# Two layers of a hybrid decoder trunk: the large SBUF tiles begin on a multiple of 2 KB

## Chip, cores and metric

The kernel runs on one NeuronCore of a Trainium2 chip. The metric is device time in microseconds of one execution: 2147.09 us before the change, the median of three runs.

## What is computed

512 tokens of width 1024 pass through two layers, all in float32. Each layer adds half a SwiGLU to x, then a mixer of three groups of heads whose inputs come from one common projection, then half of another SwiGLU. A last RMSNorm closes the trunk.

```python
for l in range(DEPTH):                                   # DEPTH = 2, D_MODEL = 1024, D_FF = 2816
    x = x + 0.5 * swiglu(rmsnorm(x, ffn1_norm[l]), ffn1_w_gate[l], ffn1_w_up[l], ffn1_w_down[l])
    z = rmsnorm(x, mix_norm[l]) @ w_in[l]
    ...
    y = jnp.concatenate([y_s5, y_hg, y_nsa], axis=-1).astype(x.dtype)
    x = x + y @ w_out[l]
    x = x + 0.5 * swiglu(rmsnorm(x, ffn2_norm[l]), ffn2_w_gate[l], ffn2_w_up[l], ffn2_w_down[l])
return rmsnorm(x, final_norm)
```

Here `swiglu(h, wg, wu, wd)` is `(silu(h @ wg) * (h @ wu)) @ wd`. The mixer's groups are a diagonal state-space model (S5), a gated linear recurrence (HGRN2) and sparse attention (NSA).

## The kernel before

Features lie on the 128 partitions and tokens along the free axis, so x is the tile `x` of 8 x 512 numbers on each partition (`consts`, L117). Products are taken to nearly the full precision of float32 by splitting both sides: a value is the sum of a part `hi` that the type float32r holds and the rest `lo`, and a product is three matmuls, hi x hi, hi x lo and lo x hi (`mm3`, lines 219 to 221). `norm_split` (L158 and L159) writes the split of x times the norm's gain into `xs`, of 2 x 8 x 512 numbers: first the eight `hi` tiles, then the eight `lo` tiles.

A weight tile comes from DRAM into one of four buffers `wraw` (L204, issued by SyncE), 4 KB on each partition; ScalarE casts it to `whi` (L213) and VectorE takes the difference to `wlo` (L214), three buffers each. Then `dense_x` runs over the eight k-tiles of 128 features: 24 matmuls of 128 rows by 512 columns with `whi` or `wlo` as the stationary operand and `xs` as the operand that streams past it, into one PSUM tile `pd`. The same three lines serve the second half of a SwiGLU, where the hidden layer `hb` (2 x 11 x 512 numbers) streams, and the mixer's output projection (`wout`), where its split results `y` stream. The last rows of the last SwiGLU (`finish`) stream 256 columns of `hb` at a time, with weights in tiles `fw` of their own.

The program goes through SwiGLU, mixer, SwiGLU for each of the two layers. A SwiGLU is done in two halves of 11 hidden tiles; each has 22 runs of `dense_x` and 8 rows of output. Beside the first SwiGLU of layer 0 and the second one VectorE computes the S5 tables of a layer from parameters; those have few matmuls, among them groups of four, L698 and L699, that stream `Rs` (256 columns) past weights `shm`. In the mixer several streams are emitted side by side, the projections (16 runs of `dense_x`), the three groups and the output projection.

SBUF addresses are given out by tile pools, one behind the other in the order in which the pools are opened, each pool as large as its buffers: first 16 KB and 128 bytes of each partition that the system and four constants take, then `res` (everything that lives through the program: gains, `x`, `xs`, the identity `idn`, small tables), `wp` (weights and norm statistics), `sm` (small columns), and behind them the pool of the stage that runs, a SwiGLU's (`r05`, `hb`, `ft`, `fw`) or the mixer's (46 buffers of 2 KB, `y` among them). `x` stands behind the gains, at 16384 + 128 + 224 = 16736, which is 8 x 2048 + 352, and `xs` 16 KB behind it.

Of the kernel before, what the change touches and what calls it, by code (L numbers as in the profile page):

```python
# [28 lines left out]
def drain(gen):  # L29
    """run a stream of steps to its end"""  # L30
    while True:
        try:
            next(gen)
        except StopIteration as e:
            return e.value


class Weave:
    """emits several streams side by side; each step tells its tensor-engine cost in us, weights share it out"""
# [7 lines left out]
    def run(self, until=None):  # L47
        """steps until stream `until` (or all) has ended"""
        while self.live:
            e = min(self.live, key=lambda t: (t[0], t[1]))  # L50
            self.now = e[0]
            try:
                e[0] += (next(e[3]) or 0.1) / e[2]
            except StopIteration:
                self.live.remove(e)
                if e[3] is until:
                    return
# [5 lines left out]
class Trunk:  # L63
    def __init__(self, ctx, tc, A):
        self.ctx, self.tc, self.nc, self.A = ctx, tc, tc.nc, A
        E = ctx.enter_context
        self.res = E(tc.tile_pool(name="res", bufs=1))
        self.wp = E(tc.tile_pool(name="wp", bufs=3))
        self.sm = E(tc.tile_pool(name="sm", bufs=8))
        self.pp = E(tc.tile_pool(name="pp", bufs=1, space=PSUM))  # L70
        self.dr = E(tc.tile_pool(name="dr", bufs=1, space=DRAM))
# [15 lines left out]
    NB = 46  # L87
    HT = ('pS', 'pv')

# [10 lines left out]
    def rsqrt(self, v, n):  # L100
        """v: AP [128, n] -> tile [128, n] holding v ** -0.5"""
        nc = self.nc
        i = self.s([128, n], "rsi", I32)
        nc.vector.tensor_scalar(i[:], v.bitcast(I32), 1, None, op0=OP.logical_shift_right)
        nc.vector.tensor_scalar(i[:], i[:], -1.0, float(0x5f3759df), op0=OP.mult, op1=OP.add)
        y = i[:].bitcast(F32)
        for _ in range(3):
            t = self.s([128, n], "rst")
            nc.vector.tensor_tensor(t[:], y, y, op=OP.mult)
            nc.vector.scalar_tensor_tensor(t[:], t[:], -0.5, v, op0=OP.mult, op1=OP.mult)  # L110
            y2 = self.s([128, n], "rsy")
            nc.vector.scalar_tensor_tensor(y2[:], t[:], 1.5, y, op0=OP.add, op1=OP.mult)
            y = y2[:]
        return y2

# [1 line left out]
    def consts(self):  # L117
# [3 lines left out]
        self.x = res.tile([128, KT, L], F32, name="x")  # L121
        self.xs = res.tile([128, 2, KT, L], F32R, name="xs")
# [26 lines left out]
    def norm_x(self, k, gi):  # L149
        """statistics of x tile k, and its split x*gain for the next products"""  # L150
        self.norm_sq(k)
        if gi is not None:
            self.norm_split(k, gi)
# [26 lines left out]
    def norm_rows(self):  # L180
        """rstd along the columns, the same on every partition"""
        nc = self.nc
        pb = self.rows(4)
        self.rbc = self.wp.tile([128, L], F32, tag="rbc", name="rbc", bufs=2)
        nc.scalar.copy(self.rbc[:], pb[:])
# [10 lines left out]
    def wload(self, src, n):  # L196
        """src: DRAM AP [128, n] -> (hi, lo) float32r tiles that add up to it exactly"""
        return self.wsplit(self.wraw(src, n), n)
# [24 lines left out]
    def dense_x(self, src, m=128, tag="pd"):  # L223
        """one tile of m output rows: sum over the 1024 features of w * (x * gain)"""
        h, lo = self.wload(src, KT * m)
        ps = self.pmt(name="pd", tag=tag)
        for k in range(KT):
            sl = slice(k * m, (k + 1) * m)
            self.mm3(ps[:m], h[:, sl], lo[:, sl], self.xs[:, 0, k], self.xs[:, 1, k], k == 0, k == KT - 1)
            if k % 2:  # L230
                yield 1.3
        return ps

# [1 line left out]
    def begin(self, fi, gi):  # L235
        """loads x and starts the first products of a SwiGLU on its tiles as they come"""
# [82 lines left out]
    def finish(self, fi, hb, r05, fp, out):  # L319
        """the last rows of the last SwiGLU and the final norm, 256 tokens after the other"""  # L320
# [41 lines left out]
    def advance(self, side, budget):  # L362
        """emits about `budget` us of a stream of vector work"""
# [39 lines left out]
    def exp_small(self, pool, x, n, name):  # L403
        """exp of [128, n] to float32's accuracy"""
# [21 lines left out]
    def params_small(self, pool):  # L426
        """S5: step sizes, exp(lambda dt) and the input gains; HGRN2: lower bounds (both layers)"""
# [19 lines left out]
        # lower bounds: cumsum(softmax) - softmax[0]  # L447
# [14 lines left out]
        # E = expm1(lr dt)  # L462
# [10 lines left out]
        # half angle w = (li dt mod 2 pi) / 2  # L473
# [26 lines left out]
        # a = mag (cos, sin); nr = Re(a) - 1  # L500
# [22 lines left out]
        def cmul(o, a, b):  # L523
            """complex product of (re, im) pairs"""
# [13 lines left out]
        # powers a^0 .. a^8, [128, n, 9]  # L538
# [10 lines left out]
        # unit phase of a^8, decay of a^8  # L549
# [18 lines left out]
    def params_layer(self, l, pool):  # L568
        """S5 matrices of a layer, to DRAM: V, Toeplitz, readout, phases"""
# [8 lines left out]
        # phases E^c, c = 0..63, of the chunk's 8 steps, layout [g, c]  # L578
        for hf in range(2):
# [9 lines left out]
            while w < 32:  # L589
                # E^(2w) = (E^w)^2, then columns 2w .. 4w-1 from 0 .. 2w-1  # L590
# [16 lines left out]
            # modulated values take [re; im] * C + [im; re] * (S, -S)  # L607
# [4 lines left out]
        # input matrices: BB = [re; im], BX = [-im; re] of g * b  # L612
# [18 lines left out]
        # readout matrices from c: D1 = [re; -im], C2 = [im; re]  # L631
# [3 lines left out]
        D1 = c1  # L635
# [3 lines left out]
        # powers in falling order, a^7 .. a^0  # L639
# [13 lines left out]
        def expand(out, X, Y, W, gsl, op):  # L653
            """out[., g, h, s] = X[., g, h] W0[., g, s] (op) Y[., g, h] W1[., g, s]"""
# [27 lines left out]
        # Toeplitz matrices of the 8 steps, from rows of the readout moved by 0 / 1 matrices  # L682
# [20 lines left out]
    def cmp_bias(self, l, pool):  # L703
        """contribution of the position vectors to the hidden layer of the block compression"""
# [38 lines left out]
    def s5_half(self, l, hf, u, U, W):  # L743
        """yields y = gelu(ssm + d u) * 2 for 8 groups, [channel, (s c)]"""
# [45 lines left out]
    def gelu2(self, y, p, n):  # L790
        """2 * gelu(y) of an SBUF AP [p, n]"""
# [12 lines left out]
    def s5_glu(self, l, y2):  # L804
# [4 lines left out]
        for m in range(2):  # L809
# [7 lines left out]
            # natural order of time, split  # L817
# [7 lines left out]
    def silu_ps(self, ps, name):  # L825
        """silu(ps * rstd)"""
# [25 lines left out]
    def hg_pair(self, l, pr, q, f, k, g, V, tag="pv"):  # L852
        """two heads; q, f, k, g: [2 x 64, t]"""
        nc = self.nc
        v = nc.vector
        # what the products of keys and queries keep: within 64 tokens, and blocks of 64, 128 and 256 to the next one
# [6 lines left out]
        def prod(K, Q, e):  # L863
            """keys against queries within each 64 tokens: [2 x 64 keys, 4, 64 queries]"""
# [15 lines left out]
        for lev in range(9):  # L880
# [16 lines left out]
            if lev < 8:  # L897
# [4 lines left out]
                # the last level reads the second half of Q and the first half of K alone  # L902
# [39 lines left out]
        # rms norm over the head's 64 values  # L942
# [29 lines left out]
    def cmp_in(self, ps):  # L972
        """[2 groups x 64, t] -> [64 | 64 shifted by one token, group, t]"""
# [14 lines left out]
    def cmp_hidden(self, l, kv, kk, w1):  # L988
        """both halves of a block in one product over its 16 tokens: rows (half, hidden), columns (group, chunk)"""
# [13 lines left out]
    def cmp_k(self, l, h2):  # L1003
        """compressed keys, stacked twice: [128, 64] with columns (group, block)"""
# [8 lines left out]
    def cmp_v(self, l, h2):  # L1013
        """compressed values, block diagonal by head pair: [4 x 32 blocks, pair, 2 x 64]"""
# [15 lines left out]
    def nsa_k(self, ps):  # L1030
        """[k_sl | k_wn] of a group -> for each: hi twice, lo twice on the partitions"""
# [15 lines left out]
    def nsa_q(self, ps):  # L1047
        """two heads -> [hi | lo] on the partitions for each, scaled, with the sign of a distance to the maximum"""
# [13 lines left out]
    def nsa_gates(self, g):  # L1062
        """sigmoid of the gates' logits, in place"""
# [5 lines left out]
    def bias_tile(self, h):  # L1069
        """row p, column c: minus the bias of distance p + 384 - c, read off along a skew of the lines of 640"""  # L1070
# [5 lines left out]
    def nsa_cmp(self, g, T, Q, kc, gates):  # L1076
        """gated and normalised weights of the compressed blocks, transposed: [4 x 32, t]"""
# [42 lines left out]
    def nsa(self, st):  # L1120
        """attention of all heads, one pipeline over (group, head pair, head, 128 queries)"""
# [16 lines left out]
        def scores(g, hp, i):  # L1138
            """weights of two heads and 128 queries, [head][selected, window]"""
# [86 lines left out]
    def dense_tok(self, W, n, name, gates=None):  # L1226
        """n columns of w_in (256, and 24 more for the gates) as [token, 4, 256]"""
# [28 lines left out]
    def row_halves(self, V):  # L1256
        """copies of V that keep tokens 0-63 / 64-127 of each 128 and hold zeros for the others"""
# [131 lines left out]
def _layout(inp):  # L1389
# [4 lines left out]
    def tiles(w, m):  # L1394
        """[K, M] -> [M / m, 128, K / 128, m]"""
        K, M = w.shape
        return w.reshape(K // 128, 128, M // m, m).transpose(2, 1, 0, 3)
# [34 lines left out]
    # S5: [2 (re / im) x 64 states, group]  # L1432
# [19 lines left out]
    # constants of the shapes  # L1452
# [40 lines left out]
```

## Time and profile before

| | |
|---|---|
| median of 3 runs | 2147.09 us |
| lowest run | 2145.63 us |
| span of the profiled execution, first to last instruction | 2143.8 us |
| TensorE busy | 2121.0 us, 99% |
| VectorE busy | 1188.3 us, 55% |
| ScalarE busy | 785.9 us, 37% |
| GpSimd busy | 82.9 us, 4% |
| DMA | 209.11 MB, mean 98 GB/s |

PE stands for TensorE's matmuls and PEld for its weight loads, DVE for VectorE, ACT for ScalarE, POOL for GpSimd and SP for SyncE. Busy time is the union of an engine's instructions. Matmuls are pipelined, so that each one's duration overlaps the next one's start: how fast they follow each other is read from their starts. In a row, `pd<-xs,whi` says that a matmul writes `pd` and streams `xs` past the weights `whi`. One run of the three took 2792.54 us; the median isn't moved by it.

### The profile page before, as it was taken

Reading aid. Unit: us, or ns where it says so; the run is one execution under the profiler, and the core shown is the slowest. Engines: PE = TensorE matmul, PEld = TensorE weight load, DVE = VectorE, ACT = ScalarE, POOL = GpSimd, SP = SyncE. Lnnn points to the kernel's source line nnn. Section 1 sums busy time; section 2 is a strip of 40 time slices with the busy share of each in tenths; the row PEclk is TensorE's granted clock in tenths of the full one; section 3 lists DMA queues with packets and bytes.
Section 4 is the critical chain, followed back from the end, with each engine's and each line's share of the span. In section 5 each row is a group of like instructions: output and inputs, shape, how many; then the busy total and the mean of one; then the engine's idle time right before and its main releaser. Section 6 shows DMA issues by size and latency. Waiting matters only on the chain.

```text
span 2143.8 us, 28943 instructions
## 1 busy us (share of the span) xinstructions
PE 2121.0 (99%) x11192; PEld 1693.9 (79%) x11192; DVE 1188.3 (55%) x2653; ACT 785.9 (37%) x1455; POOL 82.9 (4%) x153
## 2 busy tenths in 40 slices
PE   8999999999999999999999999999999999999997
PEld 6888788877767888888888888888777678888886
DVE  7864535676765864543543343366866663334335
ACT  5222223445566422222332222233455653222221
POOL 1000000111000000000000000001100000000000
PEclk9999999999999999999999999999999999999999
DMA  5334433433101432422333233234321023233322
GB/s 191 114 95 129 129 132 95 142 115 100 50 16 50 143 111 94 154 89 80 107 98 91 81 114 94 77 112 139 105 78 50 26 79 93 82 93 112 94 77 71
DMA packets 69753, 209.11 MB, mean 98 GB/s; under 512 B 9272, under 2 KB 11912, under 8 KB 69616
## 3 DMA queue, kind: packets, MB, share of 16 engines
q1 hardware_dynamic: 58192, 172.19, 26.1%
q0 software_dynamic: 11280, 35.05, 4.8%
q8 instruction: 88, 1.44, 0.3%
q14 instruction: 49, 0.40, 0.1%
q10 hardware_dynamic: 144, 0.03, 0.0%
HBM read 194.63 MB, written 15.22 MB: 98 GB/s over the span
## 4 chain that ended last, share of the span: by engine, by line
PE 96%; issue 2%; DVE 1%; DMA 0%; POOL 0%; ACT 0%; SPq 0%; DVEq 0%; POOLq 0%
PE pd L219 27%; PE pd L221 27%; PE pd L220 27%; PE pno L1193 2%; PE ppt L1177 2%; PE psS L1154 2%; PE psS L1151 1%; PE plv L870 1%; PE psc L1090 1%; PE pd L1245 1%; PE pd L1246 1%; PE pho L940 1%; PE pd L1247 1%; PE pno L1196 0%; PE pY L779 0%
## 5 line engine op out<-in xcount | busy, mean ns | idle before, releaser
L213 ACT CAST whi<-wraw 128x1024 fp32r<-128x1024 f32 (+5 forms) x377 | 344.6, 915 | 1061.0 <-PE pd L220 743.6
L219 PE MATMUL pd<-xs,whi 128*128 128x512 f32 x1664 | 666.5, 401 | 6.4 <-ACT whi L213 6.3
L221 PE MATMUL pd<-xs,wlo 128*128 128x512 f32 x1664 | 660.9, 397 | 0.0
L220 PE MATMUL pd<-xs,whi 128*128 128x512 f32 x1664 | 660.1, 397 | 0.0
L214 DVE TENSOR_TENSOR wlo<-wraw,whi 128x1024 fp32r<-128x1024 f32 (+5 forms) x377 | 396.9, 1054 | 145.2 <-ACT whi L213 137.1
L219 PEld LDWEIGHTS pd<-xs,whi 128*128 128x128 f32 x1664 | 313.4, 188 | 86.4 <-ACT whi L213 6.3
L221 PEld LDWEIGHTS pd<-xs,wlo 128*128 128x128 f32 x1664 | 312.8, 188 | 76.1 <-issue 0.4
L220 PEld LDWEIGHTS pd<-xs,whi 128*128 128x128 f32 x1664 | 313.2, 188 | 74.6 <-DVE xs L159 1.2
L219 PE MATMUL pd<-hb,whi 128*128 128x512 f32 x682 | 266.0, 390 | 0.0
L221 PE MATMUL pd<-hb,wlo 128*128 128x512 f32 x682 | 265.5, 389 | 0.0
L220 PE MATMUL pd<-hb,whi 128*128 128x512 f32 x682 | 265.4, 389 | 0.0
L288 DVE TENSOR_TENSOR ft<-ft,pd 128x512 f32<-128x512 f32 x88 | 60.4, 686 | 263.6 <-PE pd L221 263.3
L282 DVE TENSOR_TENSOR ft<-pd,rbc 128x512 f32<-128x512 f32 x88 | 60.6, 690 | 201.8 <-PE pd L221 201.8
L221 PEld LDWEIGHTS pd<-hb,wlo 128*128 128x128 f32 x682 | 128.0, 188 | 26.9
L219 PEld LDWEIGHTS pd<-hb,whi 128*128 128x128 f32 x682 | 128.1, 188 | 26.4
L220 PEld LDWEIGHTS pd<-hb,whi 128*128 128x128 f32 x682 | 128.1, 188 | 26.3
L307 DVE TENSOR_TENSOR ft<-pd,r 128x512 f32<-128x512 f32 x62 | 42.8, 691 | 109.5 <-PE pd L221 109.2
L1161 ACT ACTIVATE P<-P,mx 128x128 f32<-128x128 f32 (+3 forms) x128 | 71.7, 561 | 51.9 <-DVE mx L1157 50.2
L1157 DVE CUSTOM_DVE_ANT_0 P<-Tb,psS 128x128 f32<-128x128 f32 (+3 forms) x128 | 60.7, 484 | 49.5 <-PE psS L1154 48.8
L290 DVE TENSOR_TENSOR hb<-ft,hb 128x512 fp32r<-128x512 f32 x88 | 60.1, 683 | 0.0
L283 ACT ACTIVATE ft<-ft 128x512 f32<-128x512 f32 x88 | 55.2, 628 | 5.6 <-DVE ft L282 5.3
L289 ACT CAST hb<-ft 128x512 fp32r<-128x512 f32 x88 | 54.7, 621 | 6.5 <-DVE ft L288 4.5
(388 smaller groups left out, 2156.8 us busy)
## 6 DMA issues: line engine op xcount, KB each, us to landing
wraw<-in_gu SPq DMA_DIRECT2D x175, 512.0 KB, 3.5
wraw<-in_dn SPq DMA_DIRECT2D x64, 384.0 KB, 3.0
wraw<-in_dn SPq DMA_DIRECT2D x64, 320.0 KB, 2.8
wraw<-in_win SPq DMA_DIRECT2D x32, 512.0 KB, 3.6
w<-sp POOLq DMA_DIRECT2D x32, 256.0 KB, 6.4
wraw<-in_wo SPq DMA_DIRECT2D x32, 256.0 KB, 2.6
Tb<-tbl POOLq DMA_DIRECT2D x16, 256.0 KB, 3.5
tbl<-ext POOLq DMA_DIRECT2D x1, 2560.0 KB, 19.4
```

The source lines that it names most:

```text
L213: nc.scalar.copy(h[:, sl], w[:, sl])
L214: self.mark = nc.vector.tensor_tensor(lo[:, sl], w[:, sl], h[:, sl].bitcast(F32), op=OP.subtract)
L219: nc.tensor.matmul(ps, wh, xh, start=first, stop=False)
L220: nc.tensor.matmul(ps, wh, xl, start=False, stop=False)
L221: nc.tensor.matmul(ps, wl, xh, start=False, stop=last)
L282: nc.vector.tensor_tensor(t[:], pg[:], rbc[:], op=OP.mult)
L283: nc.scalar.activation(t[:], t[:], AF.Silu)
L288: nc.vector.tensor_tensor(t2[:], t[:], pu[:], op=OP.mult)
L289: nc.scalar.copy(hb[:, 0, f], t2[:])
L290: nc.vector.tensor_tensor(hb[:, 1, f], t2[:], hb[:, 0, f].bitcast(F32), op=OP.subtract)
L1157: v.tensor_tensor_reduce(p[:, :n], T[g][2 * hp + e][:, L - n:], ps[e][:, :n], 1.0, 1e29, OP.add, OP.min, mx[:, 2 * e + b:2 * e + b + 1])
L1161: nc.scalar.activation(P[j][:, :n], P[j][:, :n], AF.Exp, bias=mx[:, j:j + 1], scale=-1.0, accum_out=sm_[:, j:j + 1])
```

## The change

The small pool `sm` is opened right behind `res`; `x` and `xs` leave `res` for a pool of their own, `big`, behind a tile of 192 bytes that nothing reads; `wp` follows. The sizes are such that `big` then begins at 24576, a multiple of 2 KB, and as the tiles behind it are multiples of 2 KB themselves, so do all that follow.

```diff
         self.res = E(tc.tile_pool(name="res", bufs=1))
+        self.sm = E(tc.tile_pool(name="sm", bufs=8))
+        self.al = E(tc.tile_pool(name="al", bufs=1))
+        self.big = E(tc.tile_pool(name="big", bufs=1))
         self.wp = E(tc.tile_pool(name="wp", bufs=3))
-        self.sm = E(tc.tile_pool(name="sm", bufs=8))
...
     NB = 46
+    ALIGN = 192
...
-        self.x = res.tile([128, KT, L], F32, name="x")
-        self.xs = res.tile([128, 2, KT, L], F32R, name="xs")
+
+        self.al.tile([128, self.ALIGN // 4], F32, name="al")
+        self.x = self.big.tile([128, KT, L], F32, name="x")
+        self.xs = self.big.tile([128, 2, KT, L], F32R, name="xs")
```

The rest of the diff takes comments out. Instructions, their order on each engine and what each waits for are the same before and after. The start addresses in a partition, as the program gives them out, with their remainders:

| tile | before | mod 64 | mod 2048 | after | mod 64 | mod 2048 |
|---|---|---|---|---|---|---|
| `x` | 16736 | 32 | 352 | 24576 | 0 | 0 |
| `xs` | 33120 | 32 | 352 | 40960 | 0 | 0 |
| `idn` | 65888 | 32 | 352 | 16736 | 32 | 352 |
| `wraw` (first of 4) | 71232 | 0 | 1600 | 73728 | 0 | 0 |
| `whi` (first of 3) | 91712 | 0 | 1600 | 94208 | 0 | 0 |
| `wlo` (first of 3) | 104000 | 0 | 1600 | 106496 | 0 | 0 |
| `hb` | 128832 | 0 | 1856 | 129024 | 0 | 0 |
| `ft` (first of 3) | 173888 | 0 | 1856 | 174080 | 0 | 0 |
| mixer tiles, `y` among them | 126784 + 2048 n | 0 | 1856 | 126976 + 2048 n | 0 | 0 |
| `fw` (first of 4) | 184128 | 0 | 1856 | 184320 | 0 | 0 |
| `Rs`, `shm` in layer 0 | 223008, 204576 | 32 | 1824 | 223200, 204768 | 32 | 2016 |
| `Rs`, `shm` in layer 1 | 218112, 199680 | 0 | 1024 | 218304, 199872 | 0 | 1216 |

Within a tile, a slice of 512 columns begins a multiple of 2 KB behind the tile's start, and a weight slice of 128 columns a multiple of 512 bytes. The four `fw` tiles lie 5632 = 11 x 512 bytes apart.

## Rows read from the trace of the kernel before

**Rows 1.** The page's part 1 and, of its part 2, TensorE's granted clock.
```profile
PE 2121.0 (99%) x11192; PEld 1693.9 (79%) x11192; DVE 1188.3 (55%) x2653; ACT 785.9 (37%) x1455; POOL 82.9 (4%) x153
...
PEclk9999999999999999999999999999999999999999
```
**Rows 2.** The page's part 4: the chain that ended last, by engine.
```profile
PE 96%; issue 2%; DVE 1%; DMA 0%; POOL 0%; ACT 0%; SPq 0%; DVEq 0%; POOLq 0%
```
**Rows 3.** Waits: who waited for whom, us in total, times, longest.
```profile
ACT whi L213 <- PE pd L220: 743.6, 232, 5.4
...
PE pd L219 <- ACT whi L213: 6.3, 1, 6.3
```
**Rows 4.** Groups by line: xcount, busy us, mean ns of one, idle before.
```profile
L219 PE MATMUL pd<-xs,whi 128*128 128x512 f32 x1664 | 666.5, 401 | 6.4 <-ACT whi L213 6.3
L221 PE MATMUL pd<-xs,wlo 128*128 128x512 f32 x1664 | 660.9, 397 | 0.0
L220 PE MATMUL pd<-xs,whi 128*128 128x512 f32 x1664 | 660.1, 397 | 0.0
...
L219 PE MATMUL pd<-hb,whi 128*128 128x512 f32 x682 | 266.0, 390 | 0.0
L221 PE MATMUL pd<-hb,wlo 128*128 128x512 f32 x682 | 265.5, 389 | 0.0
L220 PE MATMUL pd<-hb,whi 128*128 128x512 f32 x682 | 265.4, 389 | 0.0
```
**Rows 5.** Timeline, PE: start us, us, instruction; `xs` streams.
```profile
1850.05 0.39 PE L219 MATMUL pd<-xs,whi 128*128 128x512 f32 x1
...
1852.85 0.39 PE L219 MATMUL pd<-xs,whi 128*128 128x512 f32 x1
```
**Rows 6.** The same timeline where `hb` streams.
```profile
1240.09 0.39 PE L219 MATMUL pd<-hb,whi 128*128 128x512 f32 x1
...
1242.81 0.39 PE L219 MATMUL pd<-hb,whi 128*128 128x512 f32 x1
```
**Rows 7.** The same timeline where `y` streams.
```profile
693.93 0.39 PE L219 MATMUL pd<-y,whi 128*128 128x512 f32 x1
...
696.65 0.39 PE L219 MATMUL pd<-y,whi 128*128 128x512 f32 x1
```
**Rows 8.** Windows, PE on `xs`, then on `hb`: us, busy (xcount), clock, DMA share, GB/s.
```profile
1820.00:1880.00 60.00, 60.00 (x259) 1.00 0.27 84
...
1020.00:1070.00 50.00, 50.00 (x223) 1.00 0.35 107
```
**Rows 9.** Windows, `xs`, `hb`, `y`: us, PE, PEld, DVE, ACT, POOL busy, clock, DMA.
```profile
1850.00:1853.00 3.00, 3.00 (x14) 2.40 (x14) 1.15 (x2) 1.54 (x2) 0.00 (x0) 1.00 0.28 112
1240.00:1243.00 3.00, 3.00 (x15) 2.49 (x14) 2.21 (x3) 0.84 (x1) 0.00 (x0) 1.00 0.23 77
694.00:697.00 3.00, 3.00 (x15) 2.49 (x14) 2.84 (x5) 2.15 (x4) 0.00 (x0) 1.00 0.72 186
```
**Rows 10.** Timeline, PE, layer 1: four products on `Rs`, then `hb` again.
```profile
855.80 0.28 PE L698 MATMUL ptt<-Rs,shm 128*128 128x256 f32 x1
...
856.15 0.28 PE L699 MATMUL ptt<-Rs,shm 128*128 128x256 f32 x1
856.27 0.39 PE L219 MATMUL pd<-hb,whi 128*128 128x512 f32 x1
...
857.43 0.40 PE L221 MATMUL pd<-hb,wlo 128*128 128x512 f32 x1
```
**Rows 11.** Timeline, PE, the last stage: `hb` with weights `fw`, 256 columns.
```profile
2114.10 0.28 PE L219 MATMUL pd<-hb,fw 128*128 128x256 f32 x1
...
2115.18 0.28 PE L219 MATMUL pd<-hb,fw 128*128 128x256 f32 x1
```
**Rows 12.** Timeline, PE, layer 0: four products on `Rs`.
```profile
200.18 0.28 PE L698 MATMUL ptt<-Rs,shm 128*128 128x256 f32 x1
...
200.53 0.28 PE L699 MATMUL ptt<-Rs,shm 128*128 128x256 f32 x1
```

## The prediction

> **What bounds the kernel now.** I read the page's busy shares first, then the chain that ended last, then the costliest groups, and last single stretches of the timeline and of the windows. The busy shares put TensorE at 99% of the span, at a granted clock of nine tenths or more in all 40 slices [rows 1]. The chain that ended last is 96% TensorE [rows 2]. The waits between engines say the same: ScalarE's cast of the weights waits 743.6 us in total for TensorE to give a weight buffer back, while TensorE waits for that cast once, 6.3 us, at the start [rows 3]. So DMA, ScalarE and VectorE run ahead, and what they would gain or lose by a change of a few per cent is covered. What counts is the time from one matmul's start to the next one's; I call it the pitch. The busy time of a matmul (390 to 401 ns) is no use for that, since matmuls overlap.
>
> The groups name three lines, 219 to 221, the three products of each split weight with a split operand [rows 4]. All are 128 rows by 512 columns, on the same weight tiles (`whi`, `wlo`) and the same PSUM tile (`pd`), and differ in what streams past the weights. With `xs` they take 397 to 401 ns on the average, with `hb` 389 to 390. There are 3 x 1664 = 4992 of the first and 3 x 682 = 2046 of the second; by the code another 384 (8 rows of output x 8 tiles x 3 products x 2 layers) stream `y`.
>
> The pitch shows the difference plainly. With `xs`, from the product of line 219 that starts at 1850.05 to the one at 1852.85 there are 12 steps: 2.80 us / 12 = 233.3 ns [rows 5]. With `hb`, from 1240.09 to 1242.81, also 12 steps: 2.72 / 12 = 226.7 ns [rows 6]. With `y`, from 693.93 to 696.65: again 226.7 ns [rows 7]. Over longer stretches it stays: 259 matmuls touch a window of 60 us on `xs` and 223 one of 50 us on `hb` [rows 8]; a matmul of 390 ns that overlaps an edge is counted too, so about 1.7 are to be taken off, which leaves 60 / 257.3 = 233 and 50 / 221.3 = 226 ns. Other engines don't explain it: the stretch on `xs` has the least VectorE work of the three (1.15 us in 3, against 2.21 and 2.84) and less ScalarE and DMA work than that on `y`, and it is the slow one [rows 9].
>
> What sets `xs` apart is its address. `hb` and `y` start 1,856 bytes past a multiple of 2 KB, which is a multiple of 64. `xs` starts 352 bytes past one, which is 32 past a multiple of 64, and of the operands that stream 512 columns in the dense products it alone does. The size of the difference fits: 233.3 - 226.7 = 6.6 ns, and 16 columns of 4 bytes, that is 64 bytes, at 2.4 columns per ns are 6.7 ns. My reading is that each matmul on `xs` pays for one 64-byte piece more at its ends, 33 instead of 32. No row shows the piece itself.
>
> **The change part by part.** No instruction is added, removed or moved, and no wait changes; only start addresses do. `x` and `xs` go from 32 past a multiple of 64 to a multiple of 2 KB. Weight tiles go from 64 past a multiple of 512 to a multiple of 2 KB, `hb`, `y` and the other mixer tiles from 1,856 past one to one; these were on multiples of 64 before. The small tiles and the identity keep their place within 2 KB.
>
> *`xs` as the streaming operand.* I take the row of `hb` as its price after the change. 768 of the 4992 (16 tiles x 24 products x 2 layers) stand in the mixers, the other 4224 in the SwiGLU stages, where they follow each other for long stretches: 4224 x 6.6 ns = 27.9 us. In the mixers they alternate with small products of the other streams, and there even an aligned operand doesn't always reach 226.7: behind four products of another shape `hb` takes (857.43 - 856.27) / 5 = 232 ns a step [rows 10]. So the pitch has to settle after each interruption. For the mixers the gain lies between 0 and 768 x 6.6 = 5.1 us; between ends this close I take the middle, 2.5. The sum is 30.4 us.
>
> *`hb`, `y` and the weights, from one multiple of 64 to another.* I take nothing. What bounds it: from below, nothing suggests a price yet (see the third rival); from above, the products on `Rs` and its weights, which start on multiples of 512 in layer 1, run at (856.15 - 855.80) / 3 = 117 ns for 256 columns [rows 10], those on `hb` with `fw`, 320 past a multiple of 512, at (2115.18 - 2114.10) / 9 = 120 ns [rows 11]. So 3 ns a matmul might be gained. But they come in runs of four, which may not have settled, and in layer 0, where both start 32 past a multiple of 64, four of them take the same 117 (200.18 to 200.53, 3 steps in 0.35) [rows 12]. I stay with the long row.
>
> *`x` for VectorE and ScalarE, the DMAs' targets, `ft`, `rbc`.* Nothing: a cast that waits 743.6 us for TensorE [rows 3] hides whatever these gain or lose. With that cover gone a matmul would wait for its weights, as it does now only in the first 6.3 us.
>
> When the matmuls quicken, the weights have to come quicker: a tile of 24 products is used up in 24 x 226.7 = 5.4 us, not 5.6, which against waits of this size is little. So the span goes from 2143.8 to 2113.4 us. The median of the three runs, 2147.1, is 3.3 above the span; with the same 3.3 I forecast 2116.7, rounded to **2116.5 us, 1.4% less**. Within this case, from no gain in the mixers and 10% less elsewhere to full gain and 1 ns more per matmul, it could be 2108 to 2124.
>
> The Trainium skill has a rule that speaks against this. On the page "SBUF — State Buffer", section "Specifications (TRN2)", the memory's lines are 16 bytes. By that rule an offset of 32 is no worse than one of 0, the sum would be zero and the time 2147. The rows of `xs` against `hb` and `y` disagree with it, as long as address is what parts them.
>
> **The rivals.**
>
> *No change: `xs` is slow for another reason.* The matmuls settle into one of two rhythms, and `xs` falls into the slower by something that stays, such as its place in the lower half of the partition, or the 16 KB between its two halves. (The page's rule of 16-byte lines comes out here.) For it: an aligned `hb` can also run at 232 ns for a while [rows 10], so a slow rhythm needs no misalignment; and the four products on `Rs` in layer 0, 32 off, run at 117 ns as those of layer 1 do, which aren't [rows 10, 12]. Against it: `xs` never settles over stretches of 60 us, `hb` does within some ten steps, `y`, scattered over many buffers, settles too. Time: 2147.
>
> *Faster still.* Weights and operands that all start on 2 KB let every matmul settle lower. The nearest row for how far is 117 against 120 ns [rows 10, 11], 3 ns on each of 4992 + 2046 + 384 = 7422: 22 us more, 2094. Against it: `Rs` has 117 without such a start too [rows 12]. On the page "TensorE: Matmul & The Clock Gate" of the Trainium skill, section "Back-to-back issue gap", the gap is N/2.4 + 2.5 ns, 216 for 512 columns; no row here shows it, the best being 226.7. By that rule, as an estimate, the xs products would save 17 ns and the others 11, some 114 us, and the time would be about 2033.
>
> *Slower: the two streams collide.* TensorE reads the operand and the next weights at the same time. Their starts are 288 bytes apart modulo 512 with `xs` now, 256 with `hb` and `y`; after the change all are 0 apart, since weight slices are 512 bytes. If starts at the same place get in each other's way, no stream settles. The price is read from `hb` unsettled, 232 against 226.7 ns: 2430 x 5.3 = 13 us on `hb` and `y`, and nothing gained on `xs`: 2160; with 5.3 on `xs` too, 2186. It decides from 30.4 us / 7422 = 4.1 ns per matmul on. Against it: `hb` and `fw` are 0 apart modulo 512 already, and run at 120 ns, 13.3 above 256 / 2.4 = 106.7, just as the settled 226.7 is 13.3 above 512 / 2.4 [rows 11].
>
> **How the numbers follow.** The forecast gets 0.80: three operands, two of them aligned, one difference, and its size. No change gets 0.09, faster still 0.07, collision 0.04. The forecast's own spread, 2108 to 2124, holds most of its 0.80; to reach 8 in 10 I widen it towards the neighbours, mostly down, where a small gain of the aligned streams would add to the forecast: 2098 to 2128. A measurement of this kernel tells about 2% from no change, here 43 us, 2104. Faster by over that: the second rival, 0.07, and 0.02 of the forecast's lower edge. Slower by over 2%: 0.02, the costlier half of the collision. The rest, 0.89, is within.
>
> **What would show it.** In the profile after, steps on `xs` of 226.7 ns and a mean of 389 to 390 ns for lines 219 to 221 (their numbers move by a few) would show the main step right; 233.3 would show it wrong, and with it the whole sum. `hb` and `y` should keep 226.7: less would be the second rival, 230 or more the third. TensorE should stay at 99%, and the wait of the cast for TensorE should stay in the hundreds. If `xs` reaches 226.7 and the span falls by much less than 30 us, the mixers or the supply of weights have taken it back, and TensorE's waits for `whi` would have grown.

## The result, and the profile after

The changed kernel takes 2116.97 us in the median of four runs (2116.30 to 2117.48), against 2146.49 for the kernel before in four runs (one of 2792.54, the others 2145.63 to 2147.09); the ratio is 0.9862, with an interval of 0.9848 to 0.9877. That is 1.4% less: under the 2% from which a run is called faster here, but clear of noise, as the interval lies below 1. The forecast was 2116.5. The span of the profiled execution went from 2143.8 to 2114.5 us.

The profile's page of the kernel after, parts 1 and 2 (compare [rows 1]):

```profile
span 2114.5 us, 28943 instructions
...
PE 2091.4 (99%) x11192; PEld 1695.1 (80%) x11192; DVE 1188.1 (56%) x2653; ACT 786.7 (37%) x1455; POOL 82.8 (4%) x153
```

TensorE has lost 29.6 us of busy time with the same 11192 matmuls and is still at 99%. The other engines' totals stand within 1 us. So the time came out of matmuls. Which ones, the costliest groups tell (part 5 of the same page; the changed file has five lines more ahead of the products, so lines 224 to 226 are lines 219 to 221 of before, [rows 4]):

```profile
L224 PE MATMUL pd<-xs,whi 128*128 128x512 f32 x1664 | 657.8, 395 | 6.7 <-ACT whi L218 6.1
L226 PE MATMUL pd<-xs,wlo 128*128 128x512 f32 x1664 | 652.2, 392 | 0.0
L225 PE MATMUL pd<-xs,whi 128*128 128x512 f32 x1664 | 650.8, 391 | 0.0
...
L224 PE MATMUL pd<-hb,whi 128*128 128x512 f32 x682 | 265.8, 390 | 0.0
L226 PE MATMUL pd<-hb,wlo 128*128 128x512 f32 x682 | 265.4, 389 | 0.0
L225 PE MATMUL pd<-hb,whi 128*128 128x512 f32 x682 | 265.4, 389 | 0.0
```

The three groups on `xs` have come down from 397 to 401 ns to 391 to 395; those on `hb` have not moved. What counts is the step from start to start. The timeline of TensorE in the kernel after, at three stretches (`y`, `hb`, `xs`; compare [rows 5 to 7]; start us, us, instruction):

```profile
690.14 0.39 PE L224 MATMUL pd<-y,whi 128*128 128x512 f32 x1
...
692.86 0.39 PE L224 MATMUL pd<-y,whi 128*128 128x512 f32 x1
...
1240.04 0.39 PE L224 MATMUL pd<-hb,whi 128*128 128x512 f32 x1
...
1242.76 0.39 PE L224 MATMUL pd<-hb,whi 128*128 128x512 f32 x1
...
1819.89 0.39 PE L224 MATMUL pd<-xs,whi 128*128 128x512 f32 x1
...
1822.62 0.39 PE L224 MATMUL pd<-xs,whi 128*128 128x512 f32 x1
```

Each pair is 12 steps apart. `y` and `hb` keep 2.72 / 12 = 226.7 ns. `xs` takes 2.73 / 12 = 227.5 here, where the starts are rounded to 10 ns, instead of 233.3; over its long stretches the mean step is 226.7. Summed over all starts of the trace, the steps that begin on a product with `xs` come to 1155.7 us after and 1184.6 before: 28.9 of the span's 29.3 us. All the other matmuls together differ by less than 0.3 us.

The supply keeps up. From the waits of the kernel after (who waited for whom, us in total, times, longest; compare [rows 3]):

```profile
ACT whi L218 <- PE pd L225: 703.6, 230, 5.3
...
PE pd L224 <- ACT whi L218: 6.1, 1, 6.1
```

The cast of the weights has 40 us less to wait for TensorE, and TensorE still waits for it once, at the start.

### The profile page after: what moved, and what is told of

The parts are those of the page before. It is cut to its first block, busy times and chain, and to the rows that moved or that the text cites. A ratio compares the mean times of both kernels' runs of the same rounds, so it can differ in the third digit from the quotient of the medians.

```text
span 2114.5 us, 28943 instructions
## 1 busy us (share of the span) xinstructions
PE 2091.4 (99%) x11192; PEld 1695.1 (80%) x11192; DVE 1188.1 (56%) x2653; ACT 786.7 (37%) x1455; POOL 82.8 (4%) x153
## 3 DMA queue, kind: packets, MB, share of 16 engines
q1 hardware_dynamic: 58192, 172.19, 27.1%
## 4 chain that ended last, share of the span: by engine, by line
PE 98%; DVE 1%; issue 0%; DMA 0%; ACT 0%; SPq 0%; POOL 0%; DVEq 0%; POOLq 0%
PE pd L224 28%; PE pd L226 27%; PE pd L225 27%; PE pno L1198 2%; PE ppt L1182 2%; PE psS L1159 2%; PE psS L1156 1%; PE plv L875 1%; PE pd L1250 1%; PE pd L1251 1%; PE pd L1252 1%; PE psc L1095 1%; PE pho L945 0%; PE pno L1201 0%; PE pY L784 0%
## 5 line engine op out<-in xcount | busy, mean ns | idle before, releaser
L224 PE MATMUL pd<-xs,whi 128*128 128x512 f32 x1664 | 657.8, 395 | 6.7 <-ACT whi L218 6.1
L226 PE MATMUL pd<-xs,wlo 128*128 128x512 f32 x1664 | 652.2, 392 | 0.0
L225 PE MATMUL pd<-xs,whi 128*128 128x512 f32 x1664 | 650.8, 391 | 0.0
```

Source lines behind the costliest of these rows:

```text
L224: nc.tensor.matmul(ps, wh, xh, start=first, stop=False)
L225: nc.tensor.matmul(ps, wh, xl, start=False, stop=False)
L226: nc.tensor.matmul(ps, wl, xh, start=False, stop=last)
```

## Experiments

The prediction had a mechanism (what counts is where the operand begins, modulo 64) with the right size and no row that showed it. The change moves all large tiles at once, so its success tells little about which of them mattered. In what follows a tile's start is its remainder as the table of the change gives it, and the *distance* is the start of the streaming operand minus the start of the weights it streams past. The edits that move tiles add unused tiles of 32 to 192 bytes, or resize one, and add no instruction. The kernel before is the reference in every ratio.

**Is 2 KB needed, or a multiple of 64?** In the kernel before, 32 unused bytes ahead of `x` and 32 behind `xs`. `x` and `xs` then start 384 past a multiple of 2 KB, weights 1664, `hb` and `y` 1920: all multiples of 64.

```diff
+        res.tile([128, 8], F32, name="pa")
         self.x = res.tile([128, KT, L], F32, name="x")
         self.xs = res.tile([128, 2, KT, L], F32R, name="xs")
+        res.tile([128, 8], F32, name="pb")
```

> The kernel before, with 32 unused bytes ahead of x and 32 behind xs: x and xs start on a multiple of 64 (384 past a multiple of 2 KB), all behind them moves by 64 bytes and stays off 2 KB (weights 1664 past one, hb and y 1920 past one). Theory (what counts is that the streaming operand starts on a multiple of 64): xs steps at 226.7 ns as after the change, time 2117 us, give or take 2. Rival 1 (it takes the 2 KB, for xs or for the weights beside it): xs stays at 233.3 ns, 2147 us. A value between, 2125 to 2140, would say that both count.

Measured: 2116.83 us, ratio 0.9865 (0.9850 to 0.9879). The timeline of TensorE in this kernel:

```profile
1849.91 0.39 PE L221 MATMUL pd<-xs,whi 128*128 128x512 f32 x1
...
1852.63 0.39 PE L221 MATMUL pd<-xs,whi 128*128 128x512 f32 x1
```

12 steps in 2.72 us, 226.7 ns. Starts on 2 KB are not needed: the whole gain is there without one of them.

**`xs` alone put back 32 off.** In the kernel after, with everything else where the change puts it:

```diff
-    ALIGN = 192
+    ALIGN = 128
...
+        self.big.tile([128, 8], F32, name="pa")
         self.x = self.big.tile([128, KT, L], F32, name="x")
         self.xs = self.big.tile([128, 2, KT, L], F32R, name="xs")
+        self.big.tile([128, 8], F32, name="pb")
```

> The changed kernel with xs alone 32 past a multiple of 64 (2016 past one of 2 KB); weights, hb and the mixer tiles stay on multiples of 2 KB, x on one of 64. Theory: xs steps are back at 233.3 ns and the time at 2146 us, give or take 2, hb stays at 226.7. Rival 1 (the gain comes from the weights' start, which xs only shared): xs keeps 226.7, 2117 us. Rival 2 (place in the partition): as xs stays at the same 40 KB, it keeps 226.7 as well.

Measured: 2145.29 us, ratio 0.9996 (0.9987 to 1.0006); the timeline of TensorE:

```profile
1849.70 0.40 PE L226 MATMUL pd<-xs,whi 128*128 128x512 f32 x1
...
1852.50 0.40 PE L226 MATMUL pd<-xs,whi 128*128 128x512 f32 x1
```

2.80 / 12 = 233.3 ns: the gain is gone. It hangs on where `xs` lies: the new places of the weights, `hb`, the mixer's tiles and the DMAs' targets don't bring it by themselves. In this kernel `x` has left its 2 KB as well (it starts 1984 past one, still a multiple of 64), so the next one moves `x`.

**`x` alone 32 off**, `xs` and all the rest on 2 KB:

```diff
-    ALIGN = 192
+    ALIGN = 160
...
         self.x = self.big.tile([128, KT, L], F32, name="x")
+        self.big.tile([128, 8], F32, name="pa")
         self.xs = self.big.tile([128, 2, KT, L], F32R, name="xs")
```

> The changed kernel with x alone 32 past a multiple of 64, xs and all else on 2 KB. x is read and written by VectorE, ScalarE and DMA alone. Theory: no change against the changed kernel, 2117 us, give or take 2, and the ScalarE and VectorE groups that read x (lines of norm_split, norm_sq and the residual sums) keep their means within 1%. Rival (part of the gain is x's): 2120 us or more, with longer means of these groups.

Measured: 2116.93 us, ratio 0.9865 (0.9849 to 0.9882). The groups of VectorE and ScalarE that read `x` keep their means within 0.5%: where they read it costs nothing that shows.

**The disputed cost by itself.** So far the runs agree with the prediction's reading. The next kernel measures it directly: ahead of the first SwiGLU stand 17 groups of 32 equal matmuls whose results nothing reads. This is added work, so only the groups are read, not the kernel's time.

```diff
+        for _ in R:
+            nc.tensor.matmul(ps[:], w, m[:, 0:512], **k)
...
+        for _ in R:
+            nc.tensor.matmul(ps[:], w, m[:, 8:520], **k)
...
+        for _ in R:
+            nc.tensor.matmul(ps[:, :256], w, m[:, 0:256], **k)
+        for _ in R:
+            nc.tensor.matmul(ps[:, :256], w, m[:, 8:264], **k)
+        for _ in R:
+            nc.tensor.matmul(ps[:], w8, m[:, 0:512], **k)
```

`m` is `xs`, `w` a weight slice that starts on 2 KB, `w8` one that starts 32 bytes behind it.

> The changed kernel with 17 groups of 32 equal matmuls put between the start and the first SwiGLU, whose results nothing reads; in each group the pitch of the second half is the measure. Theory (pieces of 64 bytes that the streaming operand touches, 6.67 ns each, and 13.3 ns per matmul): 512 float32r columns from a start 0 or 64 bytes past: 32 pieces, 226.7 ns; from 4, 16, 32 or 48 past: 33 pieces, 233.3 ns. 504 columns: 32 pieces from 0 and from 32 past, 226.7 ns both, though 8 columns fewer. 496 columns: 31 pieces from 0, 220.0, and 32 from 32 past, 226.7. 256 columns: 120.0 from 0 and 126.7 from 32 past. Weights that start 32 past, operand on 0: 226.7. bfloat16, 512 columns, from 0 and 32 past: 16 and 17 pieces, so at most 6.7 ns between the two. float32, 512 columns, from 0 and 32 past: the same 6.7 ns for each pass over the operand. Rival 1 (a fixed price for a start off 64): 504 columns 223.3 from 0 and 230 from 32 past. Rival 2 (the memory's 16-byte lines, the Trainium skill, SBUF - State Buffer, Specifications (TRN2)): 233.3 only from 4 past, 226.7 from 16, 32 and 48. The time grows by the groups' own, some 140 us.

The timeline of TensorE shows a group in one row, since its instructions are alike; the second column is from the first start to the last end, so that of a 512-column group less the last product's 0.39, divided by 31, gives the mean step:

```profile
40.51 7.42 PE L283 MATMUL pz<-xs,whi 128*128 128x512 f32 x32
...
62.74 7.61 PE L289 MATMUL pz<-xs,whi 128*128 128x512 f32 x32
...
77.65 7.50 PE L293 MATMUL pz<-xs,whi 128*128 128x512 f32 x32
...
84.99 7.42 PE L295 MATMUL pz<-xs,whi 128*128 128x504 f32 x32
92.25 7.42 PE L297 MATMUL pz<-xs,whi 128*128 128x504 f32 x32
...
113.75 4.00 PE L303 MATMUL pz<-xs,whi 128*128 128x256 f32 x32
117.58 3.95 PE L305 MATMUL pz<-xs,whi 128*128 128x256 f32 x32
121.36 7.63 PE L307 MATMUL pz<-xs,whi 128*128 128x512 f32 x32
```

The first is the operand at 0: (7.42 - 0.39) / 31 = 227 ns. Line 289 is the operand 32 off: 233. Line 293 is the operand 64 off: 229. By the theory 64 bytes should cost nothing, and they cost 2. Line 307 is the surprise: the operand at 0 and the *weights* 32 off, 234 ns, as slow as the other way round. At 256 columns the order turns: the operand at 0 (line 303) is slower than 32 off (line 305). A group settles in its first five to ten products, so from here on the tables give the mean step over a group's second half:

| streaming operand | columns | operand at 0 | operand 32 off |
|---|---|---|---|
| float32r | 512 | 226.7 ns | 233.2 ns |
| float32r | 504 | 226.7 | 226.7 |
| float32r | 496 | 220.0 | 224.5 |
| float32r | 256 | 120.0 | 117.8 |
| float32, each of its two passes | 512 | 429.2 | 429.2 |
| bfloat16 | 512 | 215.8 | 215.9 |

504 columns (lines 295 and 297) do what the theory of 64-byte pieces said: 226.7 ns at both starts, as much as 512 columns at 0. 496 columns 32 off were to take 226.7 and take 224.5. With 512 columns from 4 and from 16 bytes past, 233.3 was expected; 236.6 and 231.9 were measured. The float32 row says less than it seems to: its weights are `idn`, which starts at 16736, and `x` at 24576, so that the two distances are 7840 and 7872 bytes. Neither is a multiple of 256, which, as shown below, is what counts for float32r; a level pair was not tried for float32.

If a product paid for a 64-byte piece more at its ends, it would do so for 256 columns too, and the weights' start would not matter. From here on there were two theories: the operand's own start, or its distance from the weights' start. They part where both move together.

**Everything 32 off.** In the kernel before, only the 32 bytes behind `xs`: `xs` stays 32 past a multiple of 64 and weights, `hb` and `y` join it there. The distance of `xs` from the weights goes from 352 - 1600 = -1248 to 352 - 1632 = -1280, which is -5 x 256.

```diff
         self.xs = res.tile([128, 2, KT, L], F32R, name="xs")
+        res.tile([128, 8], F32, name="pb")
```

> The kernel before with 32 unused bytes behind xs: x and xs stay 32 past a multiple of 64, and now weights, hb and the mixer tiles do too. Theory 1 (the streaming operand's own start modulo 64): all three operands are off, xs, hb and y at 233.3 ns, 2147 + (2046 + half of 384) x 6.6 = 2161 us. Theory 2 (the two starts relative to each other, operand against weights, modulo 64: the last run's group with the operand on 0 and weights 32 past ran at 233.2 too): all relative starts are 0 again, 226.7 ns for all, 2117 us. Theory 3 (each of the two starts by itself): as theory 1 or slower, up to 240 ns, 2147 + 7422 x 6.6 = 2196 us.

Measured: 2116.16 us, ratio 0.9864 (0.9849 to 0.9878). The timeline of TensorE:

```profile
1850.14 0.39 PE L220 MATMUL pd<-xs,whi 128*128 128x512 f32 x1
...
1852.86 0.39 PE L220 MATMUL pd<-xs,whi 128*128 128x512 f32 x1
```

2.72 / 12 = 226.7 ns, with `xs` exactly where it was in [rows 5] at 233.3. One unused tile of 32 bytes, on the far side of `xs`, gives the whole gain. The theory of the operand's own start falls.

**The weights moved away instead.** In the kernel after, operands on multiples of 64, weight tiles 32 past one (`al2` is a pool opened right behind the weights'):

```diff
         self.wp = E(tc.tile_pool(name="wp", bufs=3))
+        self.al2 = E(tc.tile_pool(name="al2", bufs=1))
...
-    ALIGN = 192
+    ALIGN = 128
...
         self.xs = self.big.tile([128, 2, KT, L], F32R, name="xs")
+        self.big.tile([128, 8], F32, name="pa")
+        self.al2.tile([128, 8], F32, name="pb")
```

> The changed kernel with the weight buffers and norm statistics alone 32 past a multiple of 64; xs, x on multiples of 64, hb and the mixer tiles on multiples of 2 KB. Theory 1: no change, 226.7 ns and 2117 us. Theories 2 and 3: xs, hb and y all at 233.3 ns, 2147 + 14 to 16 = 2161 to 2163 us; hb with fw, which stays aligned, keeps 120.

Measured: 2159.68 us, ratio 1.0065 (1.0048 to 1.0082), slower than before. The timeline of TensorE on `hb`, where before had 226.7 ns [rows 6]:

```profile
1239.65 0.39 PE L227 MATMUL pd<-hb,whi 128*128 128x512 f32 x1
...
1242.45 0.39 PE L227 MATMUL pd<-hb,whi 128*128 128x512 f32 x1
```

and the groups of its page:

```profile
L227 PE MATMUL pd<-xs,whi 128*128 128x512 f32 x1664 | 667.2, 401 | 6.6 <-ACT whi L221 6.2 <-ACT xs L166 0.4
...
L227 PE MATMUL pd<-hb,whi 128*128 128x512 f32 x682 | 269.8, 396 | 0.0
```

Now `hb` pays too: 2.80 / 12 = 233.3 ns, and its mean has gone from 390 to 396. `hb`'s own start is a multiple of 64, the weights' is not. That settles that the two starts count together.

**Pairs of starts.** The next two kernels ask how, with groups of 32 products of 512 float32r columns as above, the operand and the weights each moved by columns (`m[:, 8:520]` is 32 bytes off, `h[:, 8:136]` too). First pairs of starts:

> The changed kernel with groups of 32 equal matmuls ahead of the first SwiGLU, float32r, 512 columns, operand and weights each at a start of 0, 16, 32, 48, 64 or more bytes past 2 KB. Theory 1: the operand's start alone: 226.7 from 0, 64, 128, 256 and 512, 233.3 from 16, 32, 48, whatever the weights' start. Theory 2: the difference of the starts modulo 64: 226.7 for equal starts (16 and 16, 32 and 32, 48 and 48), about 233 for 32 against 0, 0 against 32, 32 against 64. Theory 3: 226.7 only if both are on multiples of 64. The last run had 228.9 for 64 against 0, which none explains: repeated here beside 0 against 64, 64 against 64, and 128, 256, 512 against 0. 480 and 384 columns from 0: 213.3 and 173.3 ns, from 32 past 220 and 180. bfloat16 with alternating weights, so that they are loaded each time: if the slowdown is of loading weights beside a stream, it shows here between starts of 0 and 32 too; the last run's groups had no loads and took 215.8 at either start.

Four of the rows of TensorE's timeline, for the pairs (operand, weights) in bytes of (0, 0), (32, 0), (0, 32) and (32, 32):

```profile
39.63 7.42 PE L276 MATMUL pz<-xs,whi 128*128 128x512 f32 x32
46.88 7.63 PE L278 MATMUL pz<-xs,whi 128*128 128x512 f32 x32
54.35 7.62 PE L280 MATMUL pz<-xs,whi 128*128 128x512 f32 x32
61.81 7.45 PE L282 MATMUL pz<-xs,whi 128*128 128x512 f32 x32
```

Level pairs are fast, unlevel ones slow. The settled steps:

| operand, weights off by (bytes) | distance | step |
|---|---|---|
| 0, 0; 32, 32; 64, 64 | 0 | 226.7 ns |
| 64, 0; 96, 32 | 64 | 228.9 |
| 32, 0; 64, 32 | 32 | 233.3, 233.2 |
| 0, 32 | -32 | 233.3 |
| 0, 64; 32, 96 | -64 | 233.3 |
| 0, 16; 0, 48 | -16, -48 | 233.5, 233.3 |
| 96, 0 | 96 | 233.3 |
| 128, 0 | 128 | 232.3 |
| 256, 0; 512, 0 | 256, 512 | 226.7 |
| 16, 16 | 0 | 230.1 |
| 48, 48 | 0 | 233.3 |

The distance decides wherever both starts are multiples of 32; on 16 and 48 a level pair isn't fast. At 480 columns the steps for (0, 0) and (32, 0) are 216.7 and 219.9, at 384 they are 173.3 for both. bfloat16 with weights that alternate between two slices stays at 215.8 to 215.9 for all three pairs tried. Its trace has a weight load for each product, of 98 ns against 188 for float32r, so whether the type or the shorter load spares it is not shown. The bfloat16 groups of the run before had such loads too, 32 rows a group, where the expectation says they had none.

**A multiple of 64 that should not help.** If the distance counts, there is a place on a multiple of 64 that is as bad as before: `xs` on 2 KB, everything behind it 64 further, a distance of -64.

```diff
         self.xs = self.big.tile([128, 2, KT, L], F32R, name="xs")
+        self.big.tile([128, 16], F32, name="pa")
```

> The changed kernel with 64 unused bytes behind xs: xs stays on 2 KB, weights, hb and the mixer tiles go to 64 past one. Every large tile starts on a multiple of 64, and hb and y are level with the weights; xs alone starts 64 bytes below them (modulo 256). Theory 1 of the prediction (the operand's own start on a multiple of 64): 226.7 ns, 2117 us. Theory 2 as the groups of the last run have it (operand's start minus the weights', modulo 256; 64 below cost 233.3 ns): xs at 233.3 ns, 2146 us, give or take 2; hb at 226.7.

Measured: 2146.46 us, ratio 1.0000 (0.9991 to 1.0009); the timeline of TensorE:

```profile
1850.13 0.39 PE L225 MATMUL pd<-xs,whi 128*128 128x512 f32 x1
...
1852.93 0.39 PE L225 MATMUL pd<-xs,whi 128*128 128x512 f32 x1
```

2.80 / 12 = 233.3 ns with `xs` on a multiple of 2 KB and every other large tile on a multiple of 64: the whole gain of the change is lost by 64 unused bytes in another place.

**The other sign.** `xs` 64 past a multiple of 2 KB, everything behind it 256 past one: a distance of -192, which is 64 modulo 256.

```diff
-    ALIGN = 192
+    ALIGN = 256
...
         self.xs = self.big.tile([128, 2, KT, L], F32R, name="xs")
+        self.big.tile([128, 48], F32, name="pa")
```

> The changed kernel with xs at 64 past 2 KB and weights, hb and mixer tiles at 256 past one: xs starts 192 below the weights, which modulo 256 is 64 above. Theory 1: 226.7 ns, 2117 us. Theory 2: 228.9 ns as in the group with 64 against 0, so 4224 x 2.2 = 9 to 4992 x 2.2 = 11 us over the changed kernel, 2126 to 2128 us. If the period is not 256 but larger, something else, most likely 233.3 ns and 2146 us.

Measured: 2126.24 us, ratio 0.9906 (0.9889 to 0.9922); the timeline of TensorE:

```profile
1849.88 0.39 PE L225 MATMUL pd<-xs,whi 128*128 128x512 f32 x1
...
1852.63 0.39 PE L225 MATMUL pd<-xs,whi 128*128 128x512 f32 x1
```

2.75 / 12 = 229.2 ns (228.9 over the long stretches): the middle step of the table, in the real kernel, and about two thirds of the gain, as 233.3 - 228.9 = 4.4 of 6.6 ns would give.

**All distances.** Weights 256 bytes past a multiple of 2 KB, the operand from 0 to 512 in steps of 32, and four groups whose weights go round three slices 512 bytes apart, as the kernel's do.

> The changed kernel with groups of 32 equal matmuls ahead of the first SwiGLU, float32r, 512 columns, weights at 256 past 2 KB, operand from 0 to 512 past in steps of 32. Theory 2 with a period of 256: 226.7 ns at 0, 256 and 512 (differences -256, 0, 256), 228.9 at 64 and 320, 232.3 at 128 and 384, 233.3 at 32, 96, 192, 224, 288, 352, 448, 480; 160 and 416 open, like one another. Theory 1: 226.7 at every multiple of 64. Then four groups whose weights go round three slices 512 bytes apart, operand at 256, 288, 320, 224: as with one slice, 226.7, 233.3, 228.9, 233.3.

Of TensorE's timeline, the distances -256, -64, 0, 64, 128 and 256:

```profile
40.35 7.42 PE L276 MATMUL pz<-xs,whi 128*128 128x512 f32 x32
...
84.84 7.63 PE L288 MATMUL pz<-xs,whi 128*128 128x512 f32 x32
...
99.77 7.44 PE L292 MATMUL pz<-xs,whi 128*128 128x512 f32 x32
...
114.52 7.50 PE L296 MATMUL pz<-xs,whi 128*128 128x512 f32 x32
...
129.33 7.63 PE L300 MATMUL pz<-xs,whi 128*128 128x512 f32 x32
...
159.22 7.44 PE L308 MATMUL pz<-xs,whi 128*128 128x512 f32 x32
```

Settled, the steps are 226.7 ns at -256, 0 and 256; 228.9 at -192 and 64; and 233.1 to 234.3 at all the other multiples of 32. The pattern repeats with 256 bytes. With the weights going round, distances 0, 32 and 64 give 226.7, 233.3 and 228.9 as well. A distance of 128 gave 233.6, where the pairs above had 232.3; both are slow, and the difference isn't explained.

The distances of the kernels then read like this, with the time that goes with each:

| kernel | `xs` - weights, mod 256 | step on `xs` | `hb` - weights, mod 256 | step on `hb` | us |
|---|---|---|---|---|---|
| before | 32 | 233.3 ns | 0 | 226.7 ns | 2146.5 |
| after | 0 | 226.7 | 0 | 226.7 | 2117.0 |
| all on 64 | 0 | 226.7 | 0 | 226.7 | 2116.8 |
| all 32 off | 0 | 226.7 | 0 | 226.7 | 2116.2 |
| `xs` 32 off | 224 | 233.3 | 0 | 226.7 | 2145.3 |
| weights 64 above | 192 | 233.3 | 0 | 226.7 | 2146.5 |
| `xs` 64 above | 64 | 229.2 | 0 | 226.7 | 2126.2 |
| weights 32 off | 224 | 233.3 | 32 | 233.3 | 2159.7 |

Within each stream and each group here the float32r weight slices all start at the same place modulo 256, so the runs don't tell whether the distance that counts is from the weights that a product uses or from those loaded beside it. Why 256, why 64 above is about a third as bad as 64 below, and which reading waits for which inside the chip, no row shows; it stays open.

## Why the prediction was right, and where it was not

**The bound and the measure: right.** TensorE bounds the kernel before and after, and the step from start to start was the right number to compare. Because nothing else was near the critical path, the sum over steps became the change of the span almost one to one: 28.9 of 29.3 us.

**The main term: right in size, a little too large.** The forecast took `hb`'s 226.7 ns as the price of `xs` afterwards, and that is what the settled stretches have. The SwiGLU stages gave 27.1 us, forecast 27.9. Of their four stages the last gave 6.97 us, which is 1056 x 6.6; the others gave 6.6 to 6.9, the one that starts the program among them.

**The mixers: the middle value was high.** The 2 x 384 products on `xs` there gave 1.15 and 0.60 us, 1.75 together, where 2.5 stood for a range of 0 to 5.1. As the rows on `hb` behind a few other products had it [rows 10], the step must settle after each interruption; in the mixers it gains 2.3 ns on the average and not 6.6. Both terms together make 28.9 for 30.4. That the time is within half a microsecond of the forecast is luck: the span came out 1.1 us over the forecast's 2113.4, and the median lies 2.5 above it and not 3.3. The interruptions show in the means too: lines 224 to 226 have 391 to 395 ns on `xs` and not the 389 to 390 that were to show the main step right, as in the mixers the products on `xs` still take 405 and 407 ns on the average, in the last three SwiGLU stages 389 to 390.

**The narrow range: worked out inexactly.** 10% less on 27.9 us with nothing in the mixers gives 2122, not 2124; full gain and 1 ns more on each of the 4992 products gives 2109 (on all 7422, 2107), not 2108. Neither decided anything.

**What sets `xs` apart: the step that failed.** The prediction said "What sets `xs` apart is its address", which holds, and went on to "32 past a multiple of 64" and "one 64-byte piece more at its ends". That was the one reading for which it said that no row shows the piece. The runs put another in its place: with `xs` left 32 past a multiple of 64 the kernel is as fast as the changed one, and with `xs` on a multiple of 2 KB it can be as slow as before. So the match of 6.6 ns with 16 columns did not show such a piece; as 504 columns came out as it said, whether the match is chance stays open. That the forecast came out right in spite of this is luck: the change levels the distances too, while the same reasoning would have forecast the full gain for the kernel with `xs` 64 below the weights, which has none. The rows held the clue: in the kernel before, `hb` and `y` were 1856 - 1600 = 256 bytes from the weights, and `xs` -1248. The prediction took remainders of each start alone and then, in a rival, the distances modulo 512, by which the fast streams (256) and the changed ones (0) looked different. By 256 they are the same.

**`x`, the DMAs' targets, `hb`, `y`, the weights: nothing, as forecast.** `x` off by 32 left 2116.93. `hb` and `y` kept their steps, and ScalarE's cast still waits over 700 us for TensorE. For `hb` and `y` the reason given was not enough: they kept their steps because their distance went from 256 to 0. A move from one multiple of 64 to another is not free as such, as the run with a distance of -64 shows.

**The rivals.** That `xs` is slow for a lasting other reason falls with the first run. The Trainium skill's rule of 16-byte lines (page "SBUF — State Buffer", section "Specifications (TRN2)") stood beside it; here a shift of 32 bytes, two whole lines, moves the step by 6.6 ns, so the measurement decides against drawing from it that such a shift is free. *Faster still* rested on 117 against 120 ns for 256 columns. All of those products were level: `Rs` and `shm` lie 18432 = 72 x 256 bytes apart, `hb` and the first `fw` 55296 = 216 x 256. The 117 stood in runs of four, and the level group of 256 columns (line 303) begins with steps of 119, 119, 121, 117 and 117 too before it settles at 120.0. Settled, 117.8 comes only with an operand 32 bytes *off* the weights, and with 512 columns the sign is the other one, so it never was a promise for them. The Trainium skill's page "TensorE: Matmul & The Clock Gate", section "Back-to-back issue gap", gives 216 ns for 512 columns as the gap of a single product by itself; the bfloat16 groups have it (215.8), float32r with a weight load for each product and 512 columns does not settle below 226.7 in any run here. *Slower, the streams collide* had the right pair of quantities and the wrong sign: level starts are the best place, not the worst. Its price was nearly right, by chance, where unlevel starts were provoked: with the weights moved, 2159.68 us against the 2160 worked out there, though by another mix, since in that run the steps on `hb` are 233.3 and not 232.

## What to carry to other kernels

Where float32r products of 512 columns bound a kernel, read the step from start to start for each streaming tile. If tiles of the same shape differ, compare the distance of each from the weights modulo 256 bytes, and not only each one's own alignment; here a distance of 0 with both starts on multiples of 32 gave the full 6.6 ns on 227. Measure it for the shape at hand: a shift of 32 bytes cost 4.5 ns at 496 columns, 3.2 at 480, and nothing at 504 and 384. And when a change that sets many addresses pays, move one tile back at a time before a rule is made of it: this one looked like a rule about 2 KB, then like one about 64 bytes, and was neither.

## What the runs showed of the hardware that was not expected

- The settled step of a 512-column float32r product depends on the start of the streaming operand relative to the stationary one: 226.7 ns at a multiple of 256 bytes, 228.9 at 64 past one, 232 to 234 at the other multiples of 32 (both starts on multiples of 32).
- With 256 columns the sign turns (120.0 ns level, 117.8 at 32 apart), at 504 and 384 there is no difference (226.7 and 173.3), and bfloat16 (215.8 to 215.9) shows none at 512.
- Starts on odd multiples of 16 are not fast even when they are level: 230.1 ns at 16 and 16, 233.3 at 48 and 48.
